# Four phase boundaries of a two-block transformer written in one fixed order, and modulation rows summed in another way

## The chip, the core and the metric

The program runs on one core of a Trainium2 chip. A core has engines that run side by side and meet through semaphores: TensorE (PE in the rows, its weight loads PEld), VectorE (DVE), ScalarE (ACT), GpSimd (POOL) and SyncE (SP), which here issues nearly all DMAs. The metric is the device time of one execution in microseconds (us), as the median of several runs.

## The reference

256 tokens of width 1024 go through two blocks, all in float32. The first has a mixer (causal attention of 8 heads beside a gated linear recurrence), a residual with a normalised branch, and a convolved GELU feed-forward. The second is two modulated layers: neighbourhood attention (16 heads) and a SwiGLU feed-forward, then latent attention (MLA) and a mixture of 8 experts (MoE).

```python
x = x + rms_norm(mix, g_post_mix[l])                 # first block
h = rms_norm(x, g_pre_ffn[l])
x = x + rms_norm(ffn, g_post_ffn[l])
...
mod = c_act @ w_ada[i] + b_ada[i]                    # second block, layers i = 0, 1
sh_a, sc_a, g_a, sh_f, sc_f, g_f = jnp.split(mod, 6, axis=-1)
h = _modulate(x, sh_a, sc_a)                         # rmsnorm(x) * (1 + sc) + sh
x = x + g_a[:, None, :] * m
h = _modulate(x, sh_f, sc_f)
x = x + g_f[:, None, :] * f
```

So there are twelve modulation rows of 1024 numbers, written (layer, i) below with i = 0 to 5 in the order of the split; each is a product of one vector with a 1024 x 1024 matrix.

## The kernel before

The 256 tokens are two token tiles of 128 (t = 0, 1). Each float32 product is made of three TensorE products of a high and a low part: weights are split into `whi` (ACT, line 98) and `wlo` (DVE, line 99) by a stream `W` that walks one list of weight pieces for the whole program, and activations into `hT` high and low (lines 575 and 576). At most six split weights live at a time. `W.next()` hands out the next weight and prepares those ahead of it. `W.behind(fs, fv)` keeps the next twelve preparations behind two given instructions.

The phases are mixer, first feed-forward (`ffn1`), neighbourhood attention (`na`), second feed-forward (`ffn2`), MLA, MoE. Between two phases stands a boundary: the last projection of the old phase (line 480, `tokmm`, matmuls of 512 columns on lines 486, 487 and 489), the residual, the norm, eight transposes per token tile into `hT`, and the first products of the new phase. The first four boundaries, B1 to B4 below, end the mixer, `ffn1`, `na` and `ffn2`. At each, the last projection finishes tile 0 and then tile 1 (lines 627 and 771). The residual is `post_norm` (line 580) at B1 and B2, with a norm of the branch, and `gated` (line 602) at B3 and B4. `norm_T` (line 556) follows. A norm needs the sum of squares (ACT, line 540), a square root (ACT, line 507) and small DVE steps (lines 505 to 514). At B2 to B4 a shift is first put into the bank by matmuls on line 565 with 8 rows, and the transposes add to it (line 572); at B1 there is none (line 570).

The order of the instructions on each engine is chosen by the framework's scheduler when the program is built; it may interleave weight splits, row sums and the norm. `in_order` (line 458) pins the order on given engines; before, only the MoE uses it.

Modulation rows: the 1024 x 1024 matrix streams in through `W`, and DVE adds its eight 128-row blocks, each times its number of `c_act`, into `acc` (lines 287 and 289). `finish` (line 307) then sums `acc` over the partitions with eight matmuls against a column of ones (line 310; 16 instructions on PE), adds the bias on DVE (line 314), transposes the 8 columns (line 316) and stores the row (line 325) or splits it as a shift (line 321). Rows in `LATE` (line 266) are finished only after the last product of their phase: two at B2, three at B4. The others are finished as the stream reaches them.

PSUM has eight banks of 512 columns: four in the pool `pa`, two each in `pb` and `pc`; `pbc()` (line 218) takes from the last two in turn. The first feed-forward and the second need both tiles for their first product (256 columns, line 478); `na` begins with `tokmm` per tile, and MLA with 160-column products per tile (line 1092).

Of the kernel before, what the change touches and what calls it, by code (L numbers as in the profile page):

```python
# [188 lines left out]
def model(ctx: ExitStack, tc: tile.TileContext, A, out, cap=128):  # L189
# [76 lines left out]
    LATE = ((0, 2), (1, 5), (1, 2), (1, 3), (1, 4))  # L266
# [4 lines left out]

    def run_late():
        while late:
            fn, acc = late.pop(0)
            fn(acc)

    def plan_ada(layer, i):
# [20 lines left out]
        def before():  # L298
            if is_late:
                late.append((finish, ada_acc[0]))  # L300
            return ada_acc[0]
# [4 lines left out]

        def finish(acc):
            ps = pbc()
            for k in range(KD):
                PE.matmul(ps[:, k:k + 1], lhsT=acc[:, k * 128:(k + 1) * 128], rhs=ones.bitcast(F32)[:, 0:1],  # L310
                          start=True, stop=True)
            col = sm.tile([128, KD], F32, name="adac")
            b = vcol[:, 3, (layer * 6 + index) * KD:(layer * 6 + index + 1) * KD]
            V.scalar_tensor_tensor(col, ps[:, 0:KD], float(plus1), b, op0=OP.add, op1=OP.add)
# [116 lines left out]

    identr = cst.tile([KD, KD], F32R, name="identr")
# [63 lines left out]
    def rsqrt(ss, n, more=None):  # L496


        y = sm.tile([128, 1], F32, name="ry")
# [3 lines left out]
        if more is not None:  # L503
            e = sm.tile([128, 1], F32, name="re")
            V.tensor_scalar(e, more, 1.0 / n, EPS, OP.mult, OP.add)  # L505
            V.tensor_scalar(u, e, -0.5, None, OP.mult)  # L506
        SC.activation(y, ss, AF.Sqrt, scale=1.0 / n, bias=e)
        if more is not None:
# [6 lines left out]
        return y  # L515
# [39 lines left out]

    def norm_T(hT, scale, shift=None):
# [23 lines left out]
    def post_norm(g):  # L580
        def f(acc, t):

            junk = wk.tile([128, D], F32, name="h")
            tmp = wk.tile([128, D], F32, name="h")
            ss = {}
            for j in range(2):
                sl, so = (slice(i * 512, (i + 1) * 512) for i in (j, 1 - j))
                ss[j] = sm.tile([128, 1], F32, name="ss")
                f = SC.activation(junk[:, sl], acc[t][j], AF.Square, accum_out=ss[j])
                if t == 1 and j == 0:  # L590
                    with tc.issue_after(f.ins):
                        square(0, 1)
                V.tensor_mul(tmp[:, so], acc[t][1 - j], g[:, so])
            r = rsqrt(ss[1], D, ss[0])
            for j in range(2):
                sl = slice(j * 512, (j + 1) * 512)
                V.scalar_tensor_tensor(xres[:, t, sl], tmp[:, sl], r, xres[:, t, sl], op0=OP.mult, op1=OP.add)
                if t == 1 or j == 0:
                    square(t, j)
        return f  # L600
# [15 lines left out]
    def out_proj(oT, resid, more=0):  # L616

        acc = accs()
# [8 lines left out]
        for t in range(2):  # L627
            for k, w in ws:
                tokmm(acc, oT, k, w, False, k == KD - 1, ts=(t,))
            resid(acc, t)  # L630
# [117 lines left out]
    def ffn(hT, p, act, resid, mid=None):  # L748
# [22 lines left out]
        for t in range(2):  # L771
            for fj, w, e in last:
                tokmm(acc, fj, 0, w, False, e, ts=(t,))
            resid(acc, t)
# [4 lines left out]
    with ExitStack() as ph:  # L779
        p = ph.enter_context(tc.tile_pool(name="mix", bufs=1))  # L780
        hT = pair(p, [128, KD, S], "hT")
# [144 lines left out]
        out_proj(both, post_norm(g_post_mix))  # L926
# [4 lines left out]
    with ExitStack() as ph:  # L931
# [10 lines left out]
        norm_T(hT, g_pre_ffn)  # L942
# [16 lines left out]
        ffn(hT, p3, conv_act, post_norm(g_post_ffn), lambda: na_row.append(ada(0, 1)))  # L959
        na_row = na_row[0]  # L960
        W.flush()
        run_late()
# [4 lines left out]
    with ExitStack() as ph:  # L967
# [19 lines left out]
        load_T(0)  # L987
        g_a0 = ada(0, 2)
        norm_T(hT, na_row, ada_shift[0, 0])
        acc = accs()  # L990
        for k in range(KD):
            w = W.next()
            tokmm(acc, hT, k, w, k == 0, k == KD - 1)
# [24 lines left out]
        out_proj(oT, gated(g_a0))  # L1018
# [4 lines left out]
    with ExitStack() as ph:  # L1023
# [4 lines left out]
        late_pool.append(ph.enter_context(tc.tile_pool(name="late2", bufs=3)))  # L1028
        hT = pair(p, [128, KD, S], "hT")
        norm_T(hT, ff_row, ada_shift[0, 3])  # L1030
# [3 lines left out]
        def glu(j, pg, pu, dst):  # L1034
# [5 lines left out]
        ffn(hT, p3, glu, lambda acc, t: gated(g_f0[0])(acc, t),  # L1040
            lambda: (g_f0.append(ada(0, 5)), ml_row.append(ada(1, 1))))
        ml_row = ml_row[0]
        W.flush()
        run_late()
# [7 lines left out]
    with ExitStack() as ph:  # L1052
# [22 lines left out]
        with ExitStack() as ph2:  # L1075
            p0 = ph2.enter_context(tc.tile_pool(name="mla0", bufs=1))
            hT = pair(p0, [128, KD, S], "hT")
            norm_T(hT, ml_row, ada_shift[1, 0])
            g_a1 = ada(1, 2)
# [3 lines left out]
            ws = []  # L1083
            dn = [wk.tile([128, D], F32, name="h") for t in range(2)]
            for c0, c1, n in ((256, 384, 160), (0, 256, 256)):
                acc = [[pa()], [pa()]]
                for ts in ((0, 1), (0,), (1,)):
                    for c in range(3) if len(ts) == 2 else (3,):
# [457 lines left out]
```

## Time and profile before

| | us |
|---|---|
| median of 3 runs (range) | 1327.52 (1326.62 to 1328.47) |
| the profiled execution, its own time | 1326.26 |
| its span, first to last instruction | 1324.4 |
| PE busy / DVE busy / ACT busy | 1254.7 / 1076.9 / 846.5 |
| mean granted TensorE clock | 0.970 |

Busy time is the time in which an engine works on an instruction; for PE it counts matmuls from start to a modelled end, so that a busy PE is not a PE at its peak. The granted clock is 1.00 at 2.4 GHz and 0.50 at 1.2 GHz; a value between them in a window means that it changed within it. In a timeline, a row merges instructions of one kind in a run: start, duration of the run, count.

### The profile page before, as it was taken

The numbers are of one execution on the slowest core, as the hardware profiler recorded it, in microseconds if no ns is written. First come the engines' busy times: TensorE is split into PE (matmuls) and PEld (weight loads), VectorE is DVE, ScalarE is ACT, GpSimd is POOL, SyncE is SP. The second block draws the span as 40 slices with busy tenths as digits, with TensorE's granted clock in tenths as the row PEclk, the third lists the DMA queues.
The fourth block names the chain that finished last, engine by engine and source line by source line (L and its number), as shares of the span: only waits on it lengthen the run. The fifth ranks groups of instructions, "written<-read, shape, count | busy, mean of one in ns | idle before, by whom it ended". The sixth has DMA issues, their size and how long they took to land. (4 is left out here: it accounts for less than half of the span.)

```text
span 1324.4 us, 20099 instructions
## 1 busy us (share of the span) xinstructions
PE 1254.7 (95%) x7459; PEld 1118.0 (84%) x7459; DVE 1076.9 (81%) x1761; ACT 846.5 (64%) x1354; POOL 37.0 (3%) x68
## 2 busy tenths in 40 slices
PE   6988999999999989999998988999999999999985
PEld 6976989999798779999987667899999889988873
DVE  6796799997897496878768867988888898888976
ACT  7874456555566453434447747788778777878762
POOL 4000000000100000000000020000000000000100
PEclk9988999999899989999979998999999999999987
DMA  9844599892785287899642145999999999999980
GB/s 330 305 143 148 159 384 343 295 315 96 231 259 163 80 307 262 312 382 346 221 138 92 32 138 192 389 372 361 368 385 366 352 381 363 370 357 391 375 320 34
DMA packets 190171, 359.56 MB, mean 271 GB/s; under 512 B 15460, under 2 KB 147970, under 8 KB 189937
## 3 DMA queue, kind: packets, MB, share of 16 engines
q1 hardware_dynamic: 187361, 351.70, 75.1%
q10 hardware_dynamic: 1584, 3.91, 0.8%
q0 software_dynamic: 1120, 2.58, 0.5%
q8 instruction: 61, 1.00, 0.3%
q14 instruction: 45, 0.37, 0.1%
HBM read 351.56 MB, written 7.06 MB: 271 GB/s over the span
## 5 line engine op out<-in xcount | busy, mean ns | idle before, releaser
L99 DVE TENSOR_TENSOR wlo<-raw,whi 128x1024 fp32r<-128x1024 f32 (+2 forms) x577 | 644.5, 1155 | 126.0 <-ACT whi L98 119.0
L98 ACT CAST whi<-raw 128x1024 fp32r<-128x1024 f32 (+2 forms) x577 | 557.7, 1003 | 115.9 <-PE pa L489 30.8
L1467 PE MATMUL pa<-whi,xT 128*128 128x448 f32 x512 | 189.3, 370 | 3.8 <-ACT whi L98 3.8
L1468 PE MATMUL pa<-wlo,xT 128*128 128x448 f32 x512 | 187.0, 365 | 1.7 <-DVE wlo L99 1.7
L1469 PE MATMUL pa<-whi,xT 128*128 128x448 f32 x512 | 186.0, 363 | 0.0
L289 DVE SCALAR_TENSOR_TENSOR acc<-raw,cact,acc 128x1024 f32<-128x1024 f32 x84 | 107.2, 1276 | 2.9 <-DMA raw<-in_w_ada_dram 2.7
L1467 PEld LDWEIGHTS pa<-whi,xT 128*128 128x128 f32 x512 | 96.7, 189 | 11.9 <-ACT whi L98 4.9
L1468 PEld LDWEIGHTS pa<-wlo,xT 128*128 128x128 f32 x512 | 96.8, 189 | 9.4 <-DVE wlo L99 3.1
L1469 PEld LDWEIGHTS pa<-whi,xT 128*128 128x128 f32 x512 | 96.5, 189 | 6.4
L486 PE MATMUL pb<-whi,hTh 128*128 128x512 f32 x224 | 88.4, 395 | 0.7 <-ACT hTh L524 0.7
L487 PE MATMUL pb<-wlo,hTh 128*128 128x512 f32 x224 | 88.4, 395 | 0.1
L478 PE MATMUL pb<-hTh,whi 128*128 128x256 f32 x512 | 74.6, 289 | 1.1 <-ACT hTh L575 0.9
L478 PEld LDWEIGHTS pb<-hTh,whi 128*128 128x128 f32 x512 | 70.3, 196 | 6.0 <-ACT hTh L575 1.6
L478 PE MATMUL pb<-hTl,whi 128*128 128x256 f32 x512 | 72.4, 283 | 0.0
L478 PE MATMUL pb<-hTh,wlo 128*128 128x256 f32 x512 | 71.9, 283 | 0.0
L489 PE MATMUL pb<-whi,hTl 128*128 128x512 f32 x224 | 71.0, 395 | 0.0
L487 PE MATMUL pa<-wlo,fh 128*128 128x512 f32 x176 | 69.2, 393 | 0.6 <-DVE wlo L99 0.6
L486 PE MATMUL pa<-whi,fh 128*128 128x512 f32 x176 | 69.3, 394 | 0.0
L478 PEld LDWEIGHTS pb<-hTl,whi 128*128 128x128 f32 x512 | 66.3, 192 | 0.0
L478 PEld LDWEIGHTS pb<-hTh,wlo 128*128 128x128 f32 x512 | 66.1, 192 | 0.0
L478 PE MATMUL pc<-hTh,whi 128*128 128x256 f32 x448 | 63.8, 285 | 1.2 <-ACT whi L98 1.2
L478 PE MATMUL pc<-hTh,wlo 128*128 128x256 f32 x448 | 63.0, 283 | 0.0
(433 smaller groups left out, 2074.0 us busy)
## 6 DMA issues: line engine op xcount, KB each, us to landing
raw<-in_moe_w_gu_dram SPq DMA_DIRECT2D x128, 896.0 KB, 7.4
raw<-in_moe_w_down_dram SPq DMA_DIRECT2D x56, 1024.0 KB, 6.7
raw<-in_w_ada_dram SPq DMA_DIRECT2D x48, 1024.0 KB, 7.8
raw<-in_w_up_dram SPq DMA_DIRECT2D x22, 1024.0 KB, 9.7
raw<-in_ffn_w_gu_dram SPq DMA_DIRECT2D x22, 1024.0 KB, 6.2
raw<-in_na_w_qkv_dram SPq DMA_DIRECT2D x12, 1024.0 KB, 5.1
raw<-in_w_down_dram SPq DMA_DIRECT2D x11, 1024.0 KB, 4.8
raw<-in_ffn_w_down_dram SPq DMA_DIRECT2D x11, 1024.0 KB
```

The costliest lines, as they stand in the source:

```text
L98: self.last = self.nc.scalar.copy(h, src)
L99: self.nc.vector.tensor_sub(l, src, h.bitcast(F32))
L289: V.scalar_tensor_tensor(ada_acc[0], raw, cact[:, k:k + 1], ada_acc[0], op0=OP.mult, op1=OP.add)
L478: PE.matmul(ps, lhsT=w[:, k], rhs=x[:, k], start=n + k == 0, stop=n == 2 and k == KD - 1)
L486: PE.matmul(acc[t][j][:, :n], lhsT=xh, rhs=ws[j][0], start=first, stop=False)
L487: PE.matmul(acc[t][j][:, :n], lhsT=xh, rhs=ws[j][1], start=False, stop=False)
L489: PE.matmul(acc[t][j][:, :n], lhsT=xl, rhs=ws[j][0], start=False, stop=last)
L1467: PE.matmul(ps, lhsT=xh, rhs=wh, start=k == 0, stop=False)
L1468: PE.matmul(ps, lhsT=xh, rhs=wl, start=False, stop=False)
L1469: PE.matmul(ps, lhsT=xl, rhs=wh, start=False, stop=k == KD - 1)
```

## The change

The four boundaries go through one function, `crossing`, a generator. Its first half (residual, late rows, norm of tile 0) runs inside the old phase and its second half (transposes, tile 1, first products) inside the new one; all of it is under `in_order(PE, SC, V)`. Tile 0 is normed and transposed before tile 1's residual is finished. Where the new phase can begin on one tile (`na`, MLA), its first products on tile 0 are placed ahead of tile 1's transposes, 3 weights at B2 and 2 at B4. At B1 twelve matmuls of ones (`keep_clock`) stand there. The twelve weight preparations are now kept behind the last copies of tile 1, not of the first block of tile 0. The late rows are (0,3) at B1, (0,2) and (1,5) at B2, (1,2) at B4; they are summed with eight matmuls against a shifted column of ones that gives the row directly, plus one that adds the bias. (1,3) and (1,4) are no longer late. The seven rows left (`TURNED`) are transposed by eight PE transposes into two banks and summed by two DVE reductions.

```diff
-    LATE = ((0, 2), (1, 5), (1, 2), (1, 3), (1, 4))
+    LATE = ((0, 3), (0, 2), (1, 5), (1, 2))
+    TURNED = ((0, 0), (0, 1), (0, 5), (1, 0), (1, 1), (1, 3), (1, 4))
...
+        def sum_rows(acc, ps):
+            o = (layer * 6 + index) * KD
+            for k in range(KD):
+                PE.matmul(ps, lhsT=pick[:, 7 - k:15 - k], rhs=acc[:, k * 128:(k + 1) * 128], start=k == 0, stop=False)
+            PE.matmul(ps, lhsT=ident[0:96, o:o + KD], rhs=vrow[0:96, 3], start=False, stop=True)
...
         def finish(acc):
-            ps = pbc()
-            for k in range(KD):
-                PE.matmul(ps[:, k:k + 1], lhsT=acc[:, k * 128:(k + 1) * 128], rhs=ones.bitcast(F32)[:, 0:1],
-                          start=True, stop=True)
...
             col = sm.tile([128, KD], F32, name="adac")
+            for b in range(2):
+                ps = pbc()
+                for j in range(4):
+                    k = b * 4 + j
+                    PE.transpose(ps[:, j * 128:(j + 1) * 128], acc[:, k * 128:(k + 1) * 128], ident)
+                V.tensor_reduce(col[:, b * 4:b * 4 + 4], ps.rearrange("p (j n) -> p j n", j=4), axis=AX.X, op=OP.add)
...
+    def keep_clock(n):
+        if n:
+            ps = pbc()
+            for _ in range(n):
+                tc.keep_in_program_order(PE.matmul(ps, lhsT=ones, rhs=ones[:, None, :].to_broadcast([128, 4, 128]),
+                                                   start=True, stop=True))
...
+    def crossing(products, acc, g, scale, post):
...
+        with in_order(PE, SC, V):
+            products(0)
+            products(1)
...
+            if post:
+                square_acc(0, 0)
+                times_g(0, 1)
+                square_acc(0, 1)
+                times_g(0, 0)
+                sum_late()
+                r = acc_r(0)
+                next(r), next(r)
+                ra[0] = next(r)
+                add_x(0, 0)
+                square_acc(1, 0)
+                add_x(0, 1)
+                square(0, 0)
+                times_g(1, 1)
+                square(0, 1)
+                times_g(1, 0)
+                rx0, r1 = x_r(0), None
+                next(rx0), next(rx0)
+                square_acc(1, 1)
+                r1 = acc_r(1)
+                next(r1), next(r1)
+                rx[0] = next(rx0)
+                rows_of(0, 0)
+            else:
+                for j in range(2):
+                    times_g(0, j)
+                    add_x(0, j)
+                    square(0, j)
+                sum_late()
+                rx0 = x_r(0)
+                next(rx0), next(rx0)
+                times_g(1, 0)
+                add_x(1, 0)
+                square(1, 0)
+                rx[0] = next(rx0)
+                rows_of(0, 0)
+            hT, shift, between, fill = yield
...
+            shifts(0)
+            turn(0, 0)
+            head(0, 0)
+            if post:
+                rows_of(0, 1)
+                turn(0, 1)
+                head(0, 1)
+                ra[1] = next(r1)
+                for j in range(2):
+                    add_x(1, j)
+                    square(1, j)
+                rest(0, 0)
+                rx1 = x_r(1)
+                next(rx1), next(rx1)
+                rest(0, 1)
+            else:
+                times_g(1, 1)
+                add_x(1, 1)
+                square(1, 1)
+                rows_of(0, 1)
+                turn(0, 1)
+                rest(0, 0)
+                rx1 = x_r(1)
+                next(rx1), next(rx1)
+                head(0, 1)
+            for store in stores:
+                store()
+            shifts(1)
+            if between:
+                between()
+            keep_clock(fill)
+            rx[1] = next(rx1)
+            rows_of(1, 0)
+            rows_of(1, 1)
+            for b in range(2):
+                turn(1, b)
+                fs = head(1, b)
...
+            for b in range(2):
+                fv = rest(1, b)
+            W.behind(fs, fv)
...
-        norm_T(hT, g_pre_ffn)
+        cross.send((hT, None, None, 12))
...
+        def first_products():
+            acc.extend(accs())
+            for k in range(3):
+                ws.append(W.next(hold=W.bufs))
+                tokmm(acc, hT, k, ws[k], k == 0, False, ts=(0,))
+
+        cross.send((hT, ada_shift[0, 0], first_products, 0))
...
-        norm_T(hT, ff_row, ada_shift[0, 3])
+        cross.send((hT, ada_shift[0, 3], None, 0))
...
+            cross.send((hT, ada_shift[1, 0], first_products, 0))
```

Here `times_g` and `add_x` are the two halves of the residual (lines 593 and 597, or 608 and 609), `square_acc` is line 589, `rows_of` line 551, `turn` the transposes, `head` line 575 and `rest` line 576. `rsqrt` is cut into the same steps, handed out one at a time. `sum_late` takes a bank of `pa`.

## Rows read from the trace of the kernel before

**Rows 1.** Busy time of the engines by stage: stretch, its length, then PE, PEld, DVE, ACT and POOL busy (instructions), granted clock, DMA share, GB/s.

```profile
115.00:135.00 20.00, 14.54 (x64) 12.06 (x63) 15.40 (x42) 12.22 (x28) 0.48 (x1) 0.76 0.61 211
135.00:325.00 190.00, 187.33 (x1329) 175.89 (x1329) 164.94 (x234) 104.12 (x156) 0.00 (x0) 1.00 0.79 272
325.00:345.00 20.00, 19.08 (x96) 15.41 (x95) 16.23 (x47) 12.80 (x29) 3.66 (x12) 0.83 0.36 108
...
460.00:478.00 18.00, 13.10 (x65) 10.63 (x64) 15.70 (x32) 10.68 (x19) 0.00 (x0) 0.81 0.63 232
478.00:660.00 182.00, 182.00 (x1316) 172.35 (x1315) 143.82 (x159) 77.04 (x106) 0.00 (x0) 1.00 0.87 309
660.00:690.00 30.00, 30.00 (x164) 26.36 (x164) 18.40 (x46) 11.95 (x24) 0.00 (x0) 0.77 0.36 111
690.00:860.00 170.00, 151.59 (x854) 125.63 (x854) 135.20 (x353) 118.10 (x247) 11.12 (x12) 0.97 0.48 170
```

**Rows 2.** The same view in windows of 2 us, those in which the clock fell, and one in the MoE's beginning.

```profile
124.00:126.00 2.00, 0.00 (x0) 0.00 (x0) 1.78 (x13) 0.94 (x4) 0.00 (x0) 0.81 0.68 240
...
332.00:334.00 2.00, 2.00 (x8) 1.36 (x8) 1.98 (x13) 0.38 (x2) 1.71 (x7) 0.86 0.33 88
...
468.00:470.00 2.00, 1.31 (x8) 0.83 (x8) 1.62 (x6) 1.25 (x5) 0.00 (x0) 0.99 1.03 418
...
670.00:672.00 2.00, 2.00 (x17) 2.00 (x17) 1.26 (x3) 1.30 (x4) 0.00 (x0) 0.84 0.55 113
...
794.00:796.00 2.00, 0.00 (x0) 0.00 (x0) 2.00 (x7) 1.09 (x3) 0.93 (x1) 0.56 0.33 117
```

**Rows 3.** Timeline around B1: start, duration, engine, line, operation, count, and in brackets the idle time before it.

```profile
119.95 0.19 ACT L589 ACTIVATION_READ_ACCUMULATOR h<-pa 128x1 f32 x1
...
121.15 1.42 DVE L597 SCALAR_TENSOR_TENSOR xres<-h,ry,xres 128x512 f32<-128x512 f32 x2
...
122.16 0.61 PE L489 MATMUL pa<-whi,av 128*128 128x512 f32 x2
...
138.80 1.12 PE L478 MATMUL pc<-hTl,whi 128*128 128x256 f32 x8
139.76 0.76 PE L478 MATMUL pb<-hTh,whi 128*128 128x256 f32 x5
```

**Rows 4.** Timeline around B2.

```profile
327.67 0.61 PE L489 MATMUL pa<-whi,fl 128*128 128x512 f32 x2
...
361.22 0.62 PE L489 MATMUL pa<-whi,hTl 128*128 128x512 f32 x2
361.67 1.12 PE L478 MATMUL pb<-hTh,whi 128*128 128x256 f32 x8
```

**Rows 5.** Timeline around B3.

```profile
464.66 0.61 PE L489 MATMUL pa<-whi,oTl 128*128 128x512 f32 x2
...
470.39 3.89 ACT L98 CAST whi<-raw 128x1024 fp32r<-128x1024 f32 x4
...
472.62 1.41 DVE L551 SCALAR_TENSOR_TENSOR h<-xres,ry,bc 128x512 f32<-128x512 f32 x2
...
481.75 1.12 PE L478 MATMUL pb<-hTh,whi 128*128 128x256 f32 x8
```

**Rows 6.** Timeline around B4.

```profile
668.26 0.62 PE L489 MATMUL pa<-whi,fl 128*128 128x512 f32 x2
668.72 4.41 PE L310 MATMUL pb<-ones,acc 128*128 128x1 f32 x32
...
674.04 2.56 PE L310 MATMUL pb<-ones,acc 128*128 128x1 f32 x12
...
690.02 0.27 PE L489 MATMUL pa<-whi,hTl 128*128 128x160 f32 x1
690.13 0.32 PE L486 MATMUL pa<-whi,hTh 128*128 128x256 f32 x1
```

**Rows 7.** Single lines over the whole program: engine, operation, count, and min/median/max of one in ns.

```profile
L593 DVE TENSOR_TENSOR h<-pa,bc x8: 680/680/692, 118.7 to 330.7; 128x512 f32<-128x512 f32 x8
L575 ACT CAST hTh<-pb x10: 585/586/598, 10.5 to 684.2; 128x512 fp32r<-128x512 f32 x10
L576 DVE TENSOR_TENSOR hTl<-pb,hTh x10: 680/691/692, 11.2 to 684.8; 128x512 fp32r<-128x512 f32 x10
L643 DVE TENSOR_REDUCE mx<-pa x32: 399/414/426, 713.3 to 758.0; 128x1 f32<-128x256 f32 x32
```

**Rows 8.** Timeline: the sum of row (0,3) in the mixer and of row (0,0) in `ffn1`, four transposes and the matmul after them, and the router's products in the MoE, whose shape (8 columns of weights, 128 moving columns, float32) is that of `sum_rows`.

```profile
103.56 1.84 PE L310 MATMUL pb<-ones,acc 128*128 128x1 f32 x16
...
230.13 1.84 PE L310 MATMUL pb<-ones,acc 128*128 128x1 f32 x16
...
340.53 0.60 PE L572 MATMUL pb<-ident,h 128*128 128x128 f32 x4
340.88 0.48 PE L487 MATMUL pa<-wlo,hTh 128*128 128x512 f32 x1
...
783.96 1.92 PE L1205 MATMUL pc<-acc,wr 128*8 128x128 f32 x16 [0.24 <-ACT acc L1202]
```

**Rows 9.** Timeline in `ffn1`: the last products of a projection, and the last read of its bank by DVE.

```profile
236.02 1.12 PE L478 MATMUL pc<-hTl,whi 128*128 128x256 f32 x8
...
239.86 0.47 DVE L952 SCALAR_TENSOR_TENSOR y<-pc,vcol,y 128x254 f32<-128x254 f32 x1
```

More of the change, by code (lines that the diff above doesn't have):

```diff
@@ L299, in before @@
             if is_late:
-                late.append((finish, ada_acc[0]))
+                late.append((sum_rows, store_rows, ada_acc[0]))
             return ada_acc[0]
@@ L430, in model @@
     V.tensor_scalar(ones, ident, 0.0, 1.0, op0=OP.mult, op1=OP.add)
+    pick = cst.tile([128, 15], F32, name="pick")
+    GP.memset(pick, 0.0)
+    GP.memset(pick[:, 7:8], 1.0)
     identr = cst.tile([KD, KD], F32R, name="identr")
@@ L496, in rsqrt, with rsqrt_steps @@
     def rsqrt(ss, n, more=None):
+        steps = rsqrt_steps(ss, n, more)
+        for _ in range(2):
+            next(steps)
+        return next(steps)
+    def rsqrt_steps(ss, n, more=None):
         y = sm.tile([128, 1], F32, name="ry")
@@ L514, in rsqrt @@
         V.scalar_tensor_tensor(y, u, 1.5, y, op0=OP.add, op1=OP.mult)
[L515 removed]
+        yield y
     def sumsq(junk, src):
@@ L626, in out_proj, with products @@
                 ws.append((k, w))
-        for t in range(2):
+        def products(t):
             for k, w in ws:
                 tokmm(acc, oT, k, w, False, k == KD - 1, ts=(t,))
+        if not more:
+            W.flush()
+            return resid(products, acc)
+        for t in range(2):
+            products(t)
             resid(acc, t)
@@ L770, in ffn, with products @@
                     last.append((fj, w, j == 23))
-        for t in range(2):
+        def products(t):
             for fj, w, e in last:
                 tokmm(acc, fj, 0, w, False, e, ts=(t,))
-            resid(acc, t)
+        W.flush()
+        return resid(products, acc)
     dr_t5 = dr.tile([8, 384], F32, name="dr_t5")
@@ L925, in model @@
         g_pre_ffn = bcast(A["g_pre_ffn"])
-        out_proj(both, post_norm(g_post_mix))
+        cross = out_proj(both, lambda f, acc: crossing(f, acc, g_post_mix, g_pre_ffn, True))
+        next(cross)
     W.flush()
@@ L958, in model @@
         na_row = []
[L959 to L962, printed above, removed]
+        cross = ffn(hT, p3, conv_act, lambda f, acc: crossing(f, acc, g_post_ffn, na_row[0], True),
+                    lambda: na_row.append(ada(0, 1)))
+        next(cross)
     W.flush()
@@ L1017, in model @@
         ff_row = ada(0, 4)
-        out_proj(oT, gated(g_a0))
+        cross = out_proj(oT, lambda f, acc: crossing(f, acc, g_a0, ff_row, False))
+        next(cross)
     W.flush()
@@ L1038, in glu @@
             split_to(dst[0], dst[1], y)
[L1040 to L1044, printed above, removed]
+        cross = ffn(hT, p3, glu, lambda f, acc: crossing(f, acc, g_f0[0], ml_row[0], False),
+                    lambda: (g_f0.append(ada(0, 5)), ml_row.append(ada(1, 1))))
+        next(cross)
     W.flush()
@@ L1077, in model, with first_products @@
             hT = pair(p0, [128, KD, S], "hT")
-            norm_T(hT, ml_row, ada_shift[1, 0])
-            g_a1 = ada(1, 2)
             wr0 = accp.tile([128, D], F32, name="acc")[:, :128].rearrange("p (u k e) -> p u k e", u=2, k=KD)
             SP.dma_start(wr0[:, 0], kview(A["moe_w_router_2"][0]))
-            ws = []
+            ws, kv = [], []
+            def first_products():
+                kv.extend([[pa()], [pa()]])
+                for c in range(2):
+                    ws.append(W.next(hold=W.bufs))
+                    for kk in range(2):
+                        tokmm(kv, hT, 2 * c + kk, ws[c], c + kk == 0, False, ts=(0,), halves=1, n=160, o=kk * 416 + 256)
+            cross.send((hT, ada_shift[1, 0], first_products, 0))
+            g_a1 = ada(1, 2)
             dn = [wk.tile([128, D], F32, name="h") for t in range(2)]
             for c0, c1, n in ((256, 384, 160), (0, 256, 256)):
-                acc = [[pa()], [pa()]]
-                for ts in ((0, 1), (0,), (1,)):
-                    for c in range(3) if len(ts) == 2 else (3,):
+                acc = [[pa()], [pa()]] if c0 == 0 else kv
+                first = (((0, 1), range(3)),) if c0 == 0 else (((1,), range(2)), ((0, 1), (2,)))
+                for ts, cs in (*first, ((0,), (3,)), ((1,), (3,))):
+                    for c in cs:
                         if c == len(ws):
```

107 lines of the change are left out of this document (77 added, 30 removed).

## The prediction

> **What bounds the kernel now.** I read the stages first. The two feed-forwards are bound by PE: it is busy 187 of 190 us and 182 of 182, at full clock, while DVE has 25 and 38 us to spare and the DMA share is 0.79 and 0.87 [rows 1]. The four boundaries stand out by their clock, 0.76 to 0.83 [rows 1]. So a microsecond that PE wins at a boundary or in a feed-forward reaches the end. MLA behind B4 is looser (PE 152 of 170, and DVE 135): a gain there is passed on less surely.
>
> Then I measured each boundary in the timeline, on PE: from the moment the old phase's products have been issued to the moment at which the new ones would have begun, had they run at full speed. The second moment is found from a later one at which a known number of products is through.
> - B1: the old end is 122.16 plus two issues of 0.227 = 122.6. Two projections of 24 are through at 139.76; eight take 0.96 (138.80 to 139.76), so 48 take 5.76: 134.0. Gap 11.4 us [rows 3].
> - B2: 328.1; 96 products are through at 361.67. The last two take 0.45, so 96 take 21.8: 339.9. Gap 11.8 [rows 4].
> - B3: 465.1; 48 of 0.12 are through at 481.75: 476.0. Gap 10.9 [rows 5].
> - B4: 668.7; 48 of 0.111 are through at 690.13: 684.8. Gap 16.1, of which PE spends 4.4 + 2.6 us and more on sums of late rows (32 + 12 of 48 instructions), ahead of the norm in every queue [rows 6].
>
> **The change, part by part.** I walked the new order, each engine in order. A half-tile operation on DVE takes 0.68, started 0.61 to 0.67 after the one before, a copy on ACT 0.59 [rows 7]. From the start of the last read of a sum of squares to the first use of its root are 1.2 us (119.95 to 121.15, [rows 3]). Full clock first.
>
> B1. Tile 0's residual stays where it is. DVE then does tile 1's two products with g (122.75 to 124.0). Tile 0's squares on ACT come behind tile 1's first square, end at 124.7, and the root reaches DVE at 125.7. Tile 0's two norm rows end at 127.1, tile 1's residual at 129.2, two low parts at 130.75, tile 1's norm rows at 133.1, its second copy on ACT at 134.4. Four high products can run from 133.8, the other four wait for 134.4: a full-speed start of 134.0. That is no gain; the feed-forward needs both tiles, and in the old order the tiles overlapped as well. The row (0,3) sits in PE's idle time, 18 instructions of 1.72/16 = 0.108, 1.9 us [rows 8]. The twelve matmuls of ones take the fifth bank from `pbc`, which is the first one again, and it is free only after tile 0's first low part, at 129.8; at 0.22 they end at 132.5, just when tile 1's first half row is ready. At half clock they take 5.2 us, end at 135.0 and push the last copy to 137.6, 3 us late. So between -0.5 (shorter small steps) and +3; I take +0.5, near the full clock that the ones are there for.
>
> B2. Tile 0's rows end at 333.2. PE sums two late rows till 332.2, adds the shift, turns tile 0 by 333.9, and from 334.6 to 339.1 runs 18 products on tile 0 while DVE finishes tile 1. Tile 1 is turned at 340.0; its products follow at 340.4 with 78 of 96 left: 17.7, through at 358.1 against 361.67. That is -3.6 at full clock. At half clock from 333.4 to 340.1, as now [rows 2, 4], six of the 18 come late and the turn too: -1.2. I take -2.9, nearer the first, since PE is busy without a break here.
>
> B3. Tile 0's norm rows end at 469.8 and tile 1's at 473.0; now four weight casts (3.9 us of ACT from 470.39) and a split on DVE stand in between and tile 1's rows begin only at 472.62 [rows 5]. Those casts go behind the boundary. Copies end at 474.25, a full-speed start of 473.8: -2.2. There is no product of tile 0 and no filler between the turns; with the clock at half until 476.8 as now, -0.6. I take -0.9, near the half clock.
>
> B4. One late row instead of three: 1.9 us of PE, done at 670.6. Twelve products of 160 columns run from 675.0, tile 1 is turned at 677.45, the 36 that remain are through at 682.2 to 682.5 against 690.13: -7.5. At half clock throughout, turn at 682: -2.5. I take -5.3, between them. The three DMAs that ACT issues here now stand in its fixed order ahead of tile 0's first copy; they end at 672.4, when the first turn does, and hide behind it.
>
> Rows. A row costs PE 16 issues in 1.84 [rows 8]; eight transposes take 0.11 each (the spacing inside 340.53, [rows 8]), 0.9. (0,3) leaves the mixer, where PE is dense: -1.8, less some waiting for splits, -1.5. Five rows turned in the feed-forwards: 5 x -0.92 = -4.6. (1,3) and (1,4) move from B4 into `ffn2`: 2 x (0.9 + 0.1) = +2.0. DVE pays two reductions of 512 columns for each of the seven, no row of their own: 256 columns take 0.41, a 512-column read of a bank 0.68 [rows 7], so 1.4 a row, 2.7 us in `ffn1` and 6.8 in `ffn2`, inside the 25 and 38 spare. What may show is the banks: a row now takes three instead of two. The third is one that the running pair of projections has, and so the next projection's bank must first be emptied. I take 0.2 us a row (+1.4); the bounds are 0 and one full emptying, 236.87 to 240.33 = 3.5 [rows 9].
>
> Splits. Twelve preparations wait for the last copy. Two weights (B1, B3) or three are ready; the next is needed 5.8 us after the first product and takes 2.3 us. Hidden, with about 2 us to spare; without that cover, 2 us a boundary.
>
> Sum: 0.5 - 2.9 - 0.9 - 5.3 - 1.5 - 4.6 + 2.0 + 1.4 = **-11.3 us** on the profiled execution's 1326.26, so 1315.0. The median of the runs shown is 1.3 above that execution: **1316**.
>
> On the clock: it fell about 2.7 us after the old phase's last product at B1 and B4 (a mean of 0.81 over 124 to 126 puts the fall at 125.2) and about 5 us after it at B2 and B3, at B3 with transposes running just before; at B4 PE counts as busy all the time, on matmuls of one column [rows 2, 6]. In the MoE it fell only at 794.2, ten microseconds after the router's products, of the shape of the new sums, had begun [rows 2, 8]. So the new late sums seem to hold the clock and the old ones not. The Trainium skill, "TensorE: Matmul & The Clock Gate", Part 4, says that a transpose does not count as busy for the gate; B3's fall agrees but doesn't prove it. By that rule B1 and B3, with little but transposes, go on at half clock: 2.5 and 0.3 us less gain, 1319, inside the forecast's own range.
>
> **Rivals.**
> - *The clock holds at all four.* For it: late sums and products of tile 0 fill PE at B2 and B4. Against: B3 has neither. 0 - 3.6 - 2.2 - 7.5 - 1.8 - 4.6 + 2.0 = -17.7: **1310**.
> - *The clock falls at all four, and so the change doesn't do what its early products are for.* For it: idle stretches of 1 to 2 us stay on PE between the turns at all but B2. +3 - 1.2 - 0.6 - 2.5 and the rows -2.7 make -4.0: **1323.5**.
> - *The third bank.* The other side: each of the seven sums stalls PE until a projection's bank has been read. Price up to 3.5 a row, 24.5 in place of my 1.4: 11.8 slower, **1339**. It decides from (11.3 + 1.4)/7 = 1.8 us a row. For it: the scheduler orders by its own durations and can't see that DVE is late; DVE is the busiest engine beside PE in `ffn1`. Against: between two pairs of projections PE has 12 products of 0.23 = 2.7 us from the down projection to cover the emptying, and the scheduler may move the last transpose.
>
> **How the numbers follow.** Less than 0.2% (2.7 us) can't be told from no change here. Forecast (1312 to 1321): 0.45. Clock holds (1307 to 1312): 0.17. Clock falls (1321 to 1328): 0.26, of which 0.16 is faster by over 0.2% and 0.10 within it. Third bank: 0.12, of which 0.02 comes out within 0.2% and 0.10 slower. Faster 0.45 + 0.17 + 0.16 = 0.78, same 0.12, slower 0.10. The range of 8 in 10 leaves out the third bank's slower part (0.1), the edge of no change and the low edge of the first rival: 1308 to 1326.
>
> **What would show it.** B1 and B3: the 49th product of the new phase 134.0 + 5.8 and 475 + 5.8 less the shift of the old end; `keep_clock` beginning with tile 0's first low part. B2: the 97th 3 us nearer to the old end, clock 1.00 through it. B4: the gap down from 16.1 to about 11. `ffn1` shorter by about 1.5 us from its first product to its last, `ffn2` about the same. Wrong, if PE idles in the feed-forwards at each sum of a row, if tile 1's copies at B1 come past 135, or if the gain at B4 is gone by the first expert.

## The result and the profile after

The changed kernel takes 1318.65 us in the median of four runs (1315.56 to 1320.24), the kernel before 1327.81 in the runs beside it (1326.62 to 1328.47): ratio 0.9927, 95% interval 0.9909 to 0.9946. That is 9.2 us less where 11.3 had been forecast, and inside the forecast's own range of 1312 to 1321. The profiled execution is one of the longer ones: 1319.81, span 1317.8, 6.6 less than the span before.

The stages of the changed kernel, beside [rows 1] (stretch, length, busy time of PE, PEld, DVE, ACT and POOL, granted clock, DMA share, GB/s):

```profile
115.00:135.00 20.00, 17.66 (x95) 14.03 (x94) 15.35 (x42) 11.07 (x28) 0.48 (x1) 0.91 0.58 201
135.00:325.00 190.00, 185.97 (x1313) 174.09 (x1311) 168.04 (x241) 106.67 (x159) 0.00 (x0) 1.00 0.78 271
325.00:345.00 20.00, 19.76 (x104) 15.22 (x103) 16.04 (x44) 11.49 (x26) 3.66 (x12) 0.91 0.24 67
460.00:478.00 18.00, 15.06 (x78) 12.22 (x77) 15.13 (x31) 10.71 (x19) 0.00 (x0) 0.81 0.52 195
478.00:660.00 182.00, 182.00 (x1303) 171.46 (x1302) 151.33 (x178) 79.95 (x111) 0.00 (x0) 1.00 0.89 316
660.00:690.00 30.00, 28.57 (x144) 25.29 (x144) 21.68 (x61) 12.19 (x31) 0.00 (x0) 0.72 0.41 136
```

The feed-forwards are what they were, with 3 and 7.5 us more on DVE. B1 and B2 have more clock, B3 the same, and B4 less: 0.72 where it had been 0.77. So the boundary with the largest expected gain had less clock than before. The same view in windows of 2 us:

```profile
332.00:334.00 2.00, 2.00 (x13) 1.51 (x12) 1.90 (x6) 1.26 (x3) 1.75 (x6) 1.00 0.79 218
334.00:336.00 2.00, 2.00 (x6) 1.51 (x6) 1.93 (x9) 1.45 (x5) 0.96 (x4) 0.50 0.80 179
...
672.00:674.00 2.00, 2.00 (x10) 2.00 (x10) 1.97 (x3) 0.00 (x0) 0.00 (x0) 0.50 0.21 53
...
686.00:688.00 2.00, 2.00 (x11) 1.95 (x10) 1.21 (x6) 0.44 (x2) 0.00 (x0) 0.50 0.00 0
```

The clock was at its lower level, 1.2 of 2.4 GHz, from 334 to 337 (B2) and from 672 to 689 (B4), with PE busy nearly all the time; in front of the fall at B4 PE had idled 1.13 us. PE's timeline at B4, which answers to [rows 6]:

```profile
664.82 0.61 PE L511 MATMUL pa<-whi,fl 128*128 128x512 f32 x2
...
670.28 0.66 PE L722 MATMUL pb<-ident,h 128*128 128x128 f32 x4 [1.13 <-DVE h L651]
...
671.93 0.50 PE L508 MATMUL pa<-whi,hTh 128*128 128x160 f32 x1
...
674.57 1.05 PE L722 MATMUL pc<-ident,h 128*128 128x128 f32 x4
...
683.94 0.49 PE L508 MATMUL pa<-whi,hTh 128*128 128x256 f32 x1
```

Twelve early products take 2.6 us instead of 1.3, tile 1 is turned only at 674.57, and the 49th product starts at 683.94. Less 48 x 0.111 and the old end (665.3), that is a gap of 13.3, in place of 16.1.

I ran the changed kernel a second time, as a **control**, since its spread (4.7 us) was so much wider than that of the kernel before (1.9). In the table, all in us, are the gaps by the prediction's method and the stages between them (from the start of the product after the counted ones to the old end of the next boundary). "Best" is the combined version at the end of the next section.

| | before | forecast | changed | control | best |
|---|---|---|---|---|---|
| old end B1 | 122.6 | -1.5 | 121.1 | 121.0 | 120.8 |
| gap B1 | 11.0 | +0.5 | 11.5 | 11.2 | 11.2 |
| `ffn1` | 188.7 | -1.4 | 188.5 | 188.3 | 188.6 |
| gap B2 | 11.8 | -2.9 | 10.4 | 8.8 | 8.3 |
| attention between | 103.4 | 0 | 103.7 | 103.7 | 103.7 |
| gap B3 | 10.9 | -0.9 | 10.5 | 10.4 | 9.1 |
| `ffn2` | 187.0 | +0.2 | 186.4 | 186.4 | 186.4 |
| gap B4 | 16.1 | -5.3 | 13.3 | 10.9 | 8.1 |
| 49th product of MLA to the end | 634.3 | 0 | 633.9 | 637.2 | 635.8 |

At B1 the kernel before has a gap of 11.0 and not the 11.4 of the prediction: 51 products, not 48, were through at 139.76, since three of the third projection ran early, at half clock, as the row of seven below shows:

```profile
132.09 1.20 PE L478 MATMUL pb<-hTh,whi 128*128 128x256 f32 x4
133.09 1.05 PE L478 MATMUL pc<-hTh,whi 128*128 128x256 f32 x4
133.94 1.68 PE L478 MATMUL pb<-hTh,whi 128*128 128x256 f32 x7
```

The 49th product started at 139.40, so `ffn1` took 188.7 before.

### The profile page after: what moved, and what is told of

Its sections match the earlier page's. It is cut to its first block, busy times and chain, and to the rows that moved or that the text cites. A ratio compares the mean times of both kernels' runs of the same rounds, so it can differ in the third digit from the quotient of the medians.

```text
span 1317.8 us, 20040 instructions
## 1 busy us (share of the span) xinstructions
PE 1253.5 (95%) x7420; PEld 1113.1 (84%) x7420; DVE 1085.9 (82%) x1770; ACT 846.3 (64%) x1354; POOL 36.5 (3%) x70
## 5 line engine op out<-in xcount | busy, mean ns | idle before, releaser
L500 PEld LDWEIGHTS pb<-hTh,whi 128*128 128x128 f32 x512 | 67.4, 193 | 8.6 <-ACT whi L98 3.6
```

The source lines that it names most:

```text
L500: PE.matmul(ps, lhsT=w[:, k], rhs=x[:, k], start=n + k == 0, stop=n == 2 and k == KD - 1)
```

## The experiments

Ratios are to the kernel before on the same chip, with 95% intervals; the control's is the mark to compare with.

**Control.** No edit.

> The changed kernel once more, for its spread (four times so far lay between 1315.56 and 1320.24 us, those of the kernel before within 0.9 us of their median). Theory A (clock: the fourth boundary goes at half clock for as long as PE runs only 160-column products, whatever the run): the stretch at half clock from 672 to 689 us is there again, within 1 us, and the ratio is 0.993 again. Theory B (the clock at the boundaries differs from run to run, and that is the spread): the half-clock stretch of one boundary at least has another length by 3 us or more.

1317.46 us, 0.9932 (0.9920 to 0.9945). Theory B: B2 stays at full clock, and B4 is at the lower level for 7 us, not 17.

```profile
334.00:336.00 2.00, 2.00 (x11) 1.60 (x10) 1.86 (x10) 0.90 (x3) 0.49 (x2) 1.00 0.52 117
```

The gaps of B2 and B4 come out at 8.8 and 10.9, the forecast's -2.9 and -5.2. But the clock fell twice more behind them, at 697 to 700 and 710 to 721, and the stretch to the end is 2.9 longer than before. That the clock alone made it so is not shown: with two banks a row (below) it fell at 699 and 712, for 3.4 us each, and that stretch was 635.3. Changed kernel, control and the next run have the same instructions up to B3: B2 measured 10.4, 8.8 and 8.8. The Trainium skill, "TensorE: Matmul & The Clock Gate", Part 1, says that the same kernel shows a different number of slow matmuls from run to run, since the gate's window runs by itself and not from the kernel's start; these three traces agree that the number varies; they don't show the reason.

**Ones at B4.** Five between the two turns of tile 0, nine behind its products; `ones_fill(n)` issues n matmuls of 512 columns of ones into a spare bank that nobody reads.

```diff
                 rows_of(0, 1)
+                ones_fill(fill[0])
                 turn(0, 1)
...
-            keep_clock(fill)
+            ones_fill(fill[1])
```

> B4 alone: five 512-column matmuls of ones in PE's idle 1.1 us between the two turns of tile 0, and nine behind the early products of tile 0. Theory A (clock): granted clock 1.00 from 672 to 690 us in place of 0.50; tile 1's norm rows are ready at 673.4, its copies end near 675.5, 36 products at 0.12 us follow, so 48 products are through near 680 in place of 683.94, and the 256-column products behind them go at 0.119 in place of 0.213: 4 to 6 us earlier at the end, ratio 0.9885 to 0.990. Theory C (weights: 16 DMA engines are 0.94 to 1.02 busy between 674 and 684, and the splits of the weights start behind the last copy): the clock is 1.00 but PE waits for weights instead, the 48 products come at most 1.5 us sooner, ratio 0.992 to 0.993. Theory D (ones do not hold the clock here): windows unchanged, 14 x 0.21 to 0.43 us more on PE, ratio 0.993 to 0.995.

1316.83 us, 0.9923 (0.9910 to 0.9935). The clock held until 682, but the gap only fell to 10.5. PE's timeline, then DVE's of the same run:

```profile
672.18 2.27 PE L711 MATMUL pc<-ones 128*128 128x512 f32 x9
674.28 0.60 PE L729 MATMUL pb<-ident,h 128*128 128x128 f32 x4
```

```profile
670.80 1.42 DVE L651 SCALAR_TENSOR_TENSOR h<-xres,ry,bc 128x512 f32<-128x512 f32 x2
```

Tile 1's rows were ready at 671.5 and 672.2, and its turn stood behind my nine ones until 674.28. Neither A nor C: the clock held, but the ones took back what it gave.

**Old sums for the turned rows.**

```diff
-            for b in range(2):
-                ps = pbc()
...
-                V.tensor_reduce(col[:, b * 4:b * 4 + 4], ps.rearrange("p (j n) -> p j n", j=4), axis=AX.X, op=OP.add)
+            ps = pbc()
+            for k in range(KD):
+                PE.matmul(ps[:, k:k + 1], lhsT=acc[:, k * 128:(k + 1) * 128], rhs=ones.bitcast(F32)[:, 0:1],
+                          start=True, stop=True)
```

> The seven rows of TURNED summed by the eight one-column matmul pairs again (1.84 us of PE, one bank less, no reduction on DVE); everything else as changed. Forecast's term (0.92 us a row, less 0.2 of stalls): 0.72 a row, two rows in ffn1 and five in ffn2: 1.4 and 3.6 us longer, ratio up by 0.0038 to 0.997. Rival (stalls at banks and waits for weights ate the gain, since ffn1 measured the same length before and after the change): ffn1 and ffn2 change by less than 0.5 us each, ratio 0.993.

1322.18 us, 0.9965 (0.9952 to 0.9978). `ffn2` is 190.8 against 186.4: 4.4 for five rows, 0.87 a row, the full price without a stall. `ffn1` is 188.3 against 188.3: nothing for two rows. Waits of PE in `ffn1` (for whom, total, times, longest), the control:

```profile
PE pb L500 <- ACT whi L98: 1.5, 1, 1.5
PE pb L500 <- DVE adac L331: 1.3, 1, 1.3
PE pa L509 <- DVE wlo L99: 0.6, 1, 0.6
PE pb L500 <- DVE y L1136: 0.4, 1, 0.4
```

and with the old sums:

```profile
PE pb L498 <- ACT whi L98: 1.8, 1, 1.8
PE pa L507 <- DVE wlo L99: 0.6, 1, 0.6
```

The two waits at the sums of rows, 1.3 + 0.4, eat the 1.7 that two rows save. The kernel before has a wait at a row in `ffn1` too, one that the old sums no longer meet in the new order:

```profile
PE pc L316 <- DVE adac L314: 0.9, 1, 0.9
```

**Two banks a row.** The last small transpose goes into the second bank again.

```diff
             V.scalar_tensor_tensor(col, col, float(plus1), b, op0=OP.add, op1=OP.add)
-            ps = pbc()
             PE.transpose(ps[0:KD, 0:128], col, ident)
```

> The turned rows with two banks in place of three: the last small transpose goes into the second bank, which the reductions have read by then. Theory T (third bank: PE's two stalls in ffn1 at the sum of a row, 0.42 and 1.35 us, come from the bank that the next projections have to wait for): both stalls are gone, ffn1 is 1.3 to 1.8 us shorter from its 49th product to its last (188.3 in the changed kernel), ffn2 the same within 0.3, ratio down by 0.001 to 0.0014. Rival U (DVE is late with the reductions, 0.68 us each, whatever the bank): a stall of 1 us or more stays at the same place, ffn1 within 0.5 us of before, ratio 0.993.

1318.66 us, 0.9932 (0.9918 to 0.9946). The wait of 0.4 is gone, the other stays, now at the transpose itself:

```profile
199.23 0.27 PE L334 MATMUL pb<-ident,adac 128*8 128x128 f32 x1 [1.40 <-DVE adac L333]
```

So the small one was the third bank, the large one DVE, late with the column (rival U). `ffn1` is 186.8 here, but B1 ended late (gap 12.7), and that shortened PE's wait for whi at 165 from 1.5 to 0.3: weights set the pace there, and gave back what B1 had lost. Two other profiles with a late B1 agree (wide sums: gap 12.7, `ffn1` 186.3; ones at B3: 12.5 and 187.0). The one without ones at B1 doesn't: gap 12.9, `ffn1` 188.8, with a wait of 2.3 for DVE until 192.8 and the clock down from 193.5 to 196.9.

**Ones at B3.** Six ahead of tile 0's first turn, five between its turns, five behind tile 1's shift; the code is that of the ones at B4, with one more place.

> B3 alone: six 512-column matmuls of ones ahead of tile 0's first turn (PE idles 1.6 us there), five between its two turns (1.3 us idle), five behind the shift of tile 1. In each of the five profiles of changed kernels the clock fell at B3 between 464 and 467 us, and stayed at half for 6 to 9 us; gap 10.4 to 11.6. Theory A (clock follows PE's activity): 1.00 throughout, tile 1 turned as soon as its norm rows are there, gap 9.2 to 9.6: 1 to 2 us less, ratio 0.992 to 0.9925. Rival F (DVE's chain sets the start of ffn2, the clock hardly matters): clock 1.00, gap 10.2 or more. Rival D (ones in so short stretches do not hold it): clock 0.5 as before, gap 10.4 to 11.6 and up to 1 us more for the ones themselves.

1315.72 us, 0.9914 (0.9895 to 0.9934). The control, then this run:

```profile
466.00:468.00 2.00, 2.00 (x7) 1.21 (x5) 1.78 (x7) 0.88 (x2) 0.00 (x0) 0.50 1.02 385
```

```profile
466.00:468.00 2.00, 2.00 (x9) 1.46 (x9) 1.76 (x7) 0.77 (x2) 0.00 (x0) 1.00 1.00 385
```

Gap 9.1 in place of 10.4. Theory A: the clock was worth 1.3 us at B3. In all nine profiles of kernels with the fence but no ones at B3 it fell there, in all three with ones it held.

**No ones at B1.** The twelve are left out.

> B1 without its twelve matmuls of ones. Theory A (the ones hold or bring back the clock): PE idles from 126.5 to 130.8, the clock is at half into the first projections, as in the kernel before (0.50 until 134.5), so the 49th product comes 1 to 2 us later: gap 12.2 to 13.2 in place of 11.2 to 11.5; ratio up by 0.0008 to 0.0015. Rival I (DVE's chain alone sets the start, the clock is back by itself with the first products): gap 11.2 to 11.6, ratio unchanged.

1318.14 us, 0.9921 (0.9907 to 0.9934). Gap 12.9. PE waits 4.4 us, and its first products run at half clock:

```profile
130.71 1.12 PE L720 MATMUL pb<-ident,h 128*128 128x128 f32 x4 [4.39 <-DVE h L651]
131.62 1.06 PE L720 MATMUL pc<-ident,h 128*128 128x128 f32 x4
132.50 2.08 PE L500 MATMUL pb<-hTh,whi 128*128 128x256 f32 x8
```

Theory A for the gap. That is 1.9 more than in the kernel before: without the ones the new order is the worse one at B1. But with the twelve ones it measured 11.2 to 11.5 in six profiles and 12.5 to 12.7 in three, where the clock fell as the products began; and the time of the whole kernel does not show it.

**Wide sums.** `sum_rows` with 128 weight columns instead of 8.

```diff
-                PE.matmul(ps, lhsT=pick[:, 7 - k:15 - k], rhs=acc[:, k * 128:(k + 1) * 128], start=k == 0, stop=False)
+                PE.matmul(ps, lhsT=pick[:, 7 - k:135 - k], rhs=acc[:, k * 128:(k + 1) * 128], start=k == 0, stop=k == 7)
```

> The late sums (and that of row (0,4)) with 128 weight columns in place of 8, of which 120 are ones whose results nobody reads; same number of matmuls. Theory A1 (the clock falls behind the late sums because eight columns are little activity): B2's granted clock stays 1.00 over 334 to 338, the 18 early products go at 0.227 and end at 338.2 in place of 339.86, gap 10.4 down to 8.9; ratio 0.9915 to 0.992. Theory E (what counts is the idle PE or the stretch of time since the old phase's products, whatever the columns): the clock falls at the same place, gap unchanged, ratio 0.993. If a 128-column weight load costs more than an 8-column one, the sums take longer than 1.92 us for 16, and each boundary's later steps move by no more than that at B2 (two rows), nothing at B1 and B4, where PE idles behind them.

1317.85 us, 0.9932 (0.9919 to 0.9945). B2 held its clock, as it did in the control without the edit, so this tells nothing of columns. Its gap of 9.4 is 0.5 longer than the control's because the two late sums take 4.7 us, from 326.67 to the shift at 331.36, in place of 4.0 (326.32 to 330.36):

```profile
326.67 0.38 PE L307 MATMUL pa<-acc,ones 128*128 128x128 f32 x2
...
331.36 0.48 PE L715 MATMUL pc<-identr,shifth 8*128 8x512 f32 x1
```

Inconclusive.

**Early products, first try.** They are called behind the boundary.

```diff
-        cross.send((hT, ada_shift[0, 0], first_products, 0))
+        cross.send((hT, ada_shift[0, 0], None, 0))
+        first_products()
```

> The early products of tile 0 at B2 (18 of 512 columns) and B4 (12 of 160) run behind the whole boundary, in front of tile 1's; the rest as changed. Theory G (they are what B2 and B4 win): B2's gap at full clock is 11.7 to 12 in place of 8.8, since tile 1's rows are ready at 337.1 to 337.8, its copies at 338.9 and all 96 products come behind; B4's 1.3 (12 x 0.11) to 2.6 us longer than 10.9; ratio up by 0.003 to 0.004, 0.996 to 0.9975. Rival H (the early products only fill time in which DVE's chain would be waited for anyway, the gain is the order of the late rows): B2's and B4's gap within 1 us of 8.8 and 10.9, ratio 0.993 to 0.994.

1316.55 us, 0.9920 (0.9903 to 0.9936). It did not make them late. PE's order is free outside the boundary, and the planner put them between the turns of tile 1:

```profile
671.09 1.06 PE L722 MATMUL pc<-ident,h 128*128 128x128 f32 x4
671.80 0.48 PE L508 MATMUL pa<-whi,hTh 128*128 128x160 f32 x1
672.08 1.06 PE L722 MATMUL pb<-ident,h 128*128 128x128 f32 x4
```

The turn no longer stands behind all of them: gaps 8.3 and 8.9, shorter than the control's by 0.5 and 2.0. At B2 both held the clock. At B4 it was down for 3.4 us here and for 6.8 in the control; two profiles of the fixed order in which it was down for 3.4 (wide sums, no ones at B1) measured 9.3. So at like clock the free order is worth 0.3 at B4, and the rest of the 2.0 goes with the clock.

**Early products, second try.** They stay in the fixed order, behind the last low part.

```diff
-            if between:
-                between()
             keep_clock(fill)
...
                 fv = rest(1, b)
+            if between:
+                between()
             W.behind(fs, fv)
```

> The early products of tile 0 at B2 and B4 held back in the fixed order until both tiles are turned (in the run before, PE's order outside the boundary was free, and they still ran between the turns). Theory G (filling PE's wait between the two tiles is what the early products win, whatever the clock does): at B2 tile 1's turn comes at once when its rows are there, 11 us behind the old end, and all 96 products behind it: gap 11.5 to 12 in place of 8.3 to 8.8 at full clock; at B4 12 products of 0.11 to 0.21 us, 1.3 to 2.6 us more than 8.9 to 10.9; ratio 0.995 to 0.9965. Rival H (DVE's chain and the late rows' place are the gain): gaps within 1 us of 8.8 and 10.9, ratio 0.992 to 0.9935.

1321.00 us, 0.9948 (0.9931 to 0.9965). B2's gap is 13.5, and PE waits:

```profile
337.22 1.11 PE L722 MATMUL pc<-ident,h 128*128 128x128 f32 x4 [3.08 <-DVE h L651]
338.12 1.06 PE L722 MATMUL pb<-ident,h 128*128 128x128 f32 x4
338.84 0.78 PE L508 MATMUL pa<-whi,hTh 128*128 128x512 f32 x1
```

At B2 theory G holds: the early products are worth 4.7 there against the control, some of it the clock, which was down from 335 to 342 here; against the two profiles with the products in front in which it fell too (10.4), 3.1. The time agrees (ratio 0.9948), but its interval meets the control's. At B4 the gap is 10.0 with the clock down for 3.4 us: 0.9 less than in the control, 0.7 more than in the two profiles with as short a fall. So most of the 16.1 - 10.0 is won without them (rival H). That it is the place of the late rows is the likely reason, but not shown: no run puts the three rows back.

**No fence.**

```diff
                 fv = rest(1, b)
-            W.behind(fs, fv)
```

> The rule that twelve weight preparations wait for the boundary's last copy and last low part is taken away at all four boundaries; nothing else. Forecast (the waiting splits are hidden by the weights that are ready, and ACT's fixed order keeps casts out anyway): gaps 11.2 to 12.7, 8.8 or 10.4, 10.4 to 11.5 and 9 to 11 as in the other runs, ratio 0.993. Rival J (without it casts of 0.98 us slip in front of the copies, as in the kernel before at B3): a gap at B1 or B3 longer by 1 to 3 us, casts of L98 seen between the old end and the last copy, ratio 0.994 to 0.996. Rival K (the fence itself holds up the first weights): PE waits less for whi and wlo in the first 50 us of a phase, the wait of 1.5 us at 165 is gone, ratio 0.991 to 0.992.

1336.79 us, 1.0071 (1.0049 to 1.0093), slower than the kernel before. Gaps 14.5, 14.7, 14.0 and 14.8: 3.3, 5.9, 3.6 and 3.9 more than in the control. DVE at B2:

```profile
330.50 1.28 DVE L285 SCALAR_TENSOR_TENSOR acc<-raw,cact,acc 128x1024 f32<-128x1024 f32 x1
331.69 0.15 DVE L535 TENSOR_SCALAR ru<-re 128x1 f32<-128x1 f32 x1
331.75 1.22 DVE L99 TENSOR_TENSOR wlo<-raw,whi 128x1024 fp32r<-128x1024 f32 x1
332.88 0.15 DVE L540 SCALAR_TENSOR_TENSOR rq<-ss,ru 128x1 f32<-128x1 f32 x1
...
333.39 1.23 DVE L99 TENSOR_TENSOR wlo<-raw,whi 128x1024 fp32r<-128x1024 f32 x1
334.53 0.15 DVE L545 SCALAR_TENSOR_TENSOR ry<-ru,ry 128x1 f32<-128x1 f32 x1
```

The low parts of weights and the running sums of rows fall between the small steps of a root, and on ACT two casts stand among the squares there (330.60 and 332.32). That is rival J's mechanism, on two engines, and a longer gap at every boundary, at a larger price than it named. The order fixes the boundary's own operations against each other; it is the fence that keeps others out. The kernel before had a fence too, at tile 0's first copies; no run puts it back there, so what moving it is worth is not shown.

**Best.** Ones at B1 (seven ahead of tile 0's first turn, seventeen in place of twelve), B3 (six, five, five) and B4 (five between tile 0's turns), and the early products in PE's free order.

> Together: ones at B1 (seven ahead of tile 0's first turn, seventeen behind tile 1's shift in place of twelve), at B3 (six, five, five), at B4 (five between tile 0's turns), and the early products left to PE's free order. Theory A (what the boundaries still lose, they lose to the clock, and it is passed on): granted clock 1.00 at B1 and B3; gaps near 11.2, 8.3, 9.1 and 9 to 10; 3 to 5 us under the changed kernel's median of about 1318: ratio 0.989 to 0.991. Rival L (B1 is absorbed by the wait for weights at 165, B4 by MLA, which then loses the clock itself): the gaps are as short, but the 49th product of ffn1 moves the end of ffn1 by less than half, and the time from B4's 49th product to the end grows from 634-635 to 636-638: ratio 0.991 to 0.9925. Rival M (24 ones at half clock push tile 1's turn at B1): gap there above 13.

1314.13 us, 0.9899 (0.9879 to 0.9918). The clock held through B1, B2 and B3 and at B4 until 677, behind MLA's 49th product; in `ffn1` it was down from 165 to 169. Theory A: of the 15.3 us by which MLA's 49th product comes sooner than before, 13.8 reach the end.

**Best, with two rows of `ffn1` in the stream.**

```diff
-    TURNED = ((0, 0), (0, 1), (0, 5), (1, 0), (1, 1), (1, 3), (1, 4))
+    TURNED = ((0, 5), (1, 0), (1, 1), (1, 3), (1, 4))
```

> The combined version, with ffn1's two rows, (0,0) and (0,1), no longer turned but summed in the stream by sixteen matmuls of eight columns and two for the bias (1.95 us of PE, one bank, no reduction on DVE). Theory V (in ffn1 what a turned row saves on PE comes back as waits for DVE's reductions, 0.42 and 1.35 us): both waits are gone, ffn1 from its 49th product to its last is 188.6 plus or minus 0.4 as in the combined version, and the time is the combined version's within 1 us, ratio 0.989 to 0.991. Rival W (the waits are DVE's lateness at that place and stay, and PE's 2 us come on top): a stall of about 1 us at a row's sum, ffn1 1.5 to 2 us longer, ratio 0.991 to 0.993.

1313.85 us, 0.9896 (0.9868 to 0.9923). `ffn1` is 188.3 against 188.6 in the combined version, whose profile has the clock down in `ffn1` and one of the two waits, and 188.3 in the control, which has both and no such fall: theory V by either mark. The combined version's waits, then this run's:

```profile
PE pb L500 <- ACT whi L98: 1.7, 1, 1.7
PE pb L500 <- DVE adac L331: 1.3, 1, 1.3
```

```profile
PE pb L500 <- ACT whi L98: 1.2, 1, 1.2
PE pa L509 <- DVE wlo L99: 0.6, 1, 0.6
```

## Why the prediction was right, step by step

- **Mixer, -1.5:** -1.5 and -1.65. Right.
- **B1, +0.5:** +0.5 and +0.2, from the 11.0 that the kernel before really had; the forecast's 11.4 took 51 products for 48. The forecast had `keep_clock` wait for tile 0's first low part, at 129.8. It ran straight behind tile 0's turn (126.5; the low part came at 127.7), so the bank that it got was free. With the clock at half from 125.8 to 129.2 it ended at 130.8, before tile 1's turn. The reading of the bank failed; with it the 129.8 fell away on which the late end of +3 rested. PE's row and DVE's:

```profile
126.52 4.25 PE L592 MATMUL pb<-ones 128*128 128x512 f32 x12
```

```profile
127.66 0.68 DVE L727 TENSOR_TENSOR hTl<-pb,hTh 128x512 fp32r<-128x512 f32 x1
```

- **B2, -2.9:** -1.4 in the profile of the changed kernel, -2.9 in the control. The mechanism (tile 0's products fill PE's wait for tile 1) is shown by holding them back. The reasons given for the clock, that PE is busy without a break and that the new late sums seem to hold it, do not hold: in the first profile it fell at 334, 3 us behind these sums, with PE busy. That the number was met is luck: -2.9 was set between -3.6 for full clock and -1.2 for half, and came in an execution at full clock.
- **B3, -0.9:** -0.4 and -0.5. The half clock was foreseen; with it held the gap is -1.8, near the -2.2 that was worked out for full clock. By the Trainium skill, "TensorE: Matmul & The Clock Gate", Part 4, transposes don't count as busy in the way that other matmuls do; B3's falls agree, but the ones also filled PE's idle time, so that rule isn't shown by itself.
- **B4, -5.3:** -2.8 and -5.2. The term was set between two bounds of the clock. The changed kernel, at half clock throughout, came near the lower one (-2.5), and the control, with 6.8 us of half clock, met the term: again the draw of the clock. Over the profiles with the early products in the fixed order and no ones at B4 the gap goes with it: 13.3 with the clock down for 17 us, 10.9 to 11.0 with 6.8 (four profiles), 9.3 with 3.4 (two). The "turn at 682" does not go with the -2.5: 36 products of 0.213 behind it would end at 689.7, half a microsecond before the old 690.13. Counted from an old end at 668.7, as the walk does, the first profile's turn came at 678.0. Freeing PE's order and holding the clock gave -8.0, near the -7.5 of the full-clock bound; the order by itself is worth little (0.3 at like clock).
- **Rows, 5 x -0.92, +2.0 for two rows moved, +0.2 each for the banks:** the sum was near, the places were not. `ffn2`: forecast +0.2, measured -0.6, since no bank stalls there and a row costs the full 0.87 less. `ffn1`: forecast -1.4, measured -0.2 in the changed kernel and -0.4 in the control. This is the term that was mis-sized: 0.2 us a row for waits, where two rows lose 1.7, 0.4 by the third bank and 1.3 by DVE being late; the one wait of 0.9 that the kernel before had there is gone in return. The third rival was right about the place and far off in its price for all seven.
- **Splits, hidden:** nearly: PE's waits for weights in `ffn1` are 1.5 and 0.6, against 1.2 and 0.6 before. But the fence was only weighed for what it may cost. What having one saves, 3 to 6 us a boundary, was taken for granted in every gap that I walked.
- **A gain at B4 is passed on less surely:** over the thirteen profiles of changed kernels the time from MLA's 49th product to the end lies between 633.9 and 637.4 (before 634.3), mean 635.4. About one us of the gain goes there; why is open.
- **Left out:** the sum of row (0,4) in the attention between B2 and B3 takes the new form too; that stretch is 0.2 longer.

The changed kernel's profile misses the sum by 4.7 us: 2.5 at B4, 1.5 at B2 and 0.5 at B3, where the clock was down, 1.2 in `ffn1` and 0.3 between B2 and B3, less 0.8 in `ffn2` and 0.4 behind B4. The control's misses it by 3.3, of which 2.9 lie behind B4 and 1.0 in `ffn1`. In both are `ffn1`, half a microsecond at B3 and the 0.8; the rest is the draw of the clock, or can't be told from it. So the median's 9.2 lies near the 11.3 by an account of B2 and B4 that holds at either clock, and by luck: errors of either sign, and draws that fell between the bounds. Of the rivals, "the clock falls at all four" describes the profiled execution at three boundaries (-1.2, -0.6 and -2.5 against -1.4, -0.4 and -2.8), but not at B1, where its +3 came out as +0.5; the forecast describes the control at B2 and B4. "The third bank" is refuted at the price that it needed: `ffn2`'s five rows cost no stall.

## What to carry to other kernels

A fixed order of the boundary's own operations isn't enough; what belongs to the next phase has to be kept out of every engine's queue until the last copy, and here that fence is worth more than the order's fine points: without it each boundary is 3.3 to 5.9 us longer, and the changed kernel is slower than the one before. In such an order don't put anything long in front of the step that the next phase waits for: early products and filler matmuls belong in the wait, and should end before it does. A saving on the bounding engine is paid out only where the engine that takes over the work has time at that spot; a stage's average doesn't tell.

## What was not expected of the hardware

- The granted clock at a boundary is not a property of the kernel. With the same instructions it was at the lower level for 17 us at B4 in one execution and for 7 in the next. The changed kernel's ten runs spread over 4.9 us (1315.56 to 1320.42); the clock has part in it, but not the whole: the two longest have the lowest mean clock (0.972), the third (1320.17) one of the highest (0.976). A single profile of such a place is one draw.
- PE counted as busy nearly without a break from 672 to 689, on products of 160 and 256 columns, and the clock stayed at its lower level. The same products ran at the upper level, 0.11 us apart and not 0.21, where the clock had not fallen before. Why it took so long to rise there is open.
